# The first matmul of both MLPs as seven half-sized products, with the weights stationary, interleaved with the second matmul

## The chip, the cores and the metric

The kernel runs on one core of a Trainium2 chip, as one launch. The metric is the time of one execution on the device in microseconds (us), lower is better. Before the change three runs took 1429.39 to 1430.68 us, median 1429.62 us. A profile of one execution shows each engine: TensorE (PE, with its weight loads as PEld), VectorE (DVE), ScalarE (ACT), GpSimd (POOL) and the DMA queues that SyncE (SP) and GpSimd feed.

## The reference

A two-layer encoder over 512 positions of width 1024, in float32. Layer 0 mixes tokens with dilated sliding-window attention in three head groups, layer 1 with multi-head latent attention. Each mixer is followed by a squared-ReLU MLP:

```python
def rms_norm(x, gain):
    y = xf * lax.rsqrt(jnp.mean(xf * xf, axis=-1, keepdims=True) + EPS)
    return (y * gain.astype(jnp.float32)).astype(x.dtype)

def sq_relu_mlp(h, w1, w2):
    a = jax.nn.relu(h @ w1)
    return (a * a) @ w2

for i in range(DEPTH):                      # DEPTH = 2
    h = rms_norm(x, norm_mix[i])
    x = x + (dilated_mixer(h, ...) if i % 2 == 0 else mla_mixer(h, ...))
    h = rms_norm(x, norm_ffn[i])
    x = x + sq_relu_mlp(h, ffn_w1[i], ffn_w2[i])   # w1 1024 x 4096, w2 4096 x 1024
```

The change is in how `h @ w1` is computed, with what it needs around it.

## The kernel before

**Float32 by three matmuls.** Every float32 operand of a projection is split into two float32r parts: ACT copies the rounded part `hi`, DVE subtracts to get `lo` (lines 157 and 158 for raw weights, 795 and 796 for the weights of the second matmul, 757 and 758 for its other operand). A product is then hi.hi + hi.lo + lo.hi, three matmuls into one PSUM bank. The tiles `whi` and `wlo` have four buffers of 128x1024, `raw` has three.

**Order.** The kernel is written with a tile framework: all loops are unrolled, and a planner with a cost model decides, at build time, the order of instructions on each engine, as far as the dependences and the free buffers allow. Each engine then works strictly in that order, and the semaphores follow from it. The order in the source acts as priority. `tc.issue_after(ins)` makes what a block puts on the engine of `ins` come after `ins` there.

**The start of an MLP.** `project` (line 909) multiplies the mixer's output by its out-projection in two column halves. As each of the four token blocks of the second half ends, DVE adds it to the residual (line 915), and `norm_tile` (line 214) takes the mean square (ACT), the root (POOL), the scaled rows (DVE, line 220) and eight transposes (PE, line 124), and splits the result into `hT` (lines 228 and 229).

**The MLP** (`mlp`, line 868) takes the 4096 hidden columns in four chunks of 1024. `up(ch, grp)` computes 512 hidden columns, transposed: the weights are stationary, 128 columns at a time, and all 512 tokens stream past, so a group is 4 x 8 x 3 = 96 matmuls of 512 columns. The first group of each MLP goes by token halves (256 columns, 192 matmuls), since the halves become ready one after the other. ACT applies ReLU and squares (lines 891, 892) into `a2`. There are eight groups in a layer.

`down(ch)` calls `wino` (line 761), the second matmul for one chunk. It views the 512 x 1024 by 1024 x 1024 product as 2 x 2 blocks and uses seven products in place of eight (Winograd's form of Strassen's scheme). A product is 24 matmuls of 512 columns (line 852) with the activations stationary. Sums of activation blocks are made on DVE (line 789), sums of weight blocks by accumulating DMAs on POOL's queue (line 781), and the products are added to the residual by DVE (line 826). The weight blocks lie in four slots of `wqs`. The last chunk has its own order of products, so that token blocks end early.

The source order is up(ch+1, 0), down(ch), up(ch+1, 1); the planner sets few matmuls of the one between those of the other.

**The v projection** of layer 0 (`v_phase`, line 307 on) already uses the seven products for its weights in `piece`: sums of weight blocks are made there on DVE by `add_block` (line 334), the splits are at lines 386, 387, 406 and 407, the matmuls at line 421, the results go through `put` (lines 438, 440, 444).

**The last pair of heads** of layer 1 (`score`, lines 1114 to 1121): scores on PE, maximum on DVE, Exp on ACT. The matmuls of the out-projection's first half that need only earlier heads are set between by the planner.

Of the kernel before, what the change touches and what calls it, by code (L numbers as in the profile page):

```python
# [87 lines left out]
def encoder_kernel(ctx: ExitStack, tc: tile.TileContext, x, norm_mix, norm_ffn, a_w_qkv, a_q_gain, a_k_gain,  # L88
# [7 lines left out]
    def nm(s):  # L96
        uid[0] += 1
        return f"{s}_{uid[0]}"
# [208 lines left out]
    def v_phase(vp):  # L307
# [447 lines left out]
    def split_a(x, pool):  # L755
        t = pool.tile([P, 4, 2, 256], F32R, tag="asp", name=nm("asp"), bufs=4)
        A.activation(t[:, :, 0], x, AF.Copy)
        V.tensor_tensor(t[:, :, 1], x, t[:, :, 0].bitcast(F32), op=ALU.subtract)
        return t

    def wino(tag, Aq, w, wqs, pool, resid, done=None):
# [24 lines left out]
        def stmp(name, x, y, op):  # L786
            if name not in S:
                S[name] = pool.tile([P, 4, 256], F32, tag="S", name=nm("S"), bufs=2)
            V.tensor_tensor(S[name], x, y, op=op)
            return S[name]  # L790
# [14 lines left out]
        b7 = fetch(s7, (1, 1), add=True)  # L805

        def operands(p):
            if p == 5:
                return stmp("c", Aq(1, 0), Aq(1, 1), ALU.subtract), bT
            if p == 1:  # L810
                return Aq(0, 0), b1
            if p == 3:
                stmp("d", S["c"], Aq(0, 0), ALU.subtract)
                return stmp("c", S["d"], Aq(0, 1), ALU.add), b3
            if p == 6:
                return S["d"], fetch(sT, (1, 1), add=True)
            if p == 7:
                return stmp("c", Aq(0, 0), Aq(1, 0), ALU.subtract), b7
# [10 lines left out]

        banks = {}  # L830
        for p, chain, first, (i, n, op) in ORDER if done is None else ORDER_LAST:
            a, wq = operands(p)
            at = split_a(a, pool)
# [20 lines left out]
            put(i, n, op, bk)  # L854


    SLOTS = [(0, 1, 2, 3)]
    for _ in range(3):
# [3 lines left out]
    ORDER = [(1, "a", True, (0, 0, ALU.add)), (5, "b", True, (1, 1, ALU.add)), (3, "b", False, (0, 1, ALU.add)),  # L862
             (6, "a", False, (0, 1, ALU.subtract)), (2, "d", True, (0, 0, ALU.add)),
             (7, "a", False, (1, 1, ALU.subtract)), (4, "a", False, (1, 0, ALU.add))]

    ORDER_LAST = [ORDER[0], ORDER[4]] + ORDER[1:4] + ORDER[5:]

    def mlp(layer, w1, w2, hT_m, resid, pool, done):
        a2s = {}

        wqs = big.tile([P, 8, 2, 512], F32, tag="hT", name=nm("wqs"))

        def up(ch, grp):
            if grp == 0:
                if ch % 2:
                    a2s[ch] = pool.tile([P, 8, S], F32, tag="a2", name=nm("a2"))
                else:
                    a2s[ch] = x16.tile([P, 8, S], F32, tag="x16", name=nm("a2"))
            a2 = a2s[ch]
            c0 = ch * 1024 + grp * 512  # L880
            first = c0 == 0

            def mm(o, kt, hi, lo, hv, n=256 if first else 512):
                wh, wl = hi[:, o * P:(o + 1) * P], lo[:, o * P:(o + 1) * P]
                sl = slice(hv * n, hv * n + n)
                hh, hl = hT_m[:, kt, 0, sl], hT_m[:, kt, 1, sl]
                return [(wh, hh, sl), (wh, hl, sl), (wl, hh, sl)]

            def evac(o, acc):
                f = grp * 4 + o  # L890
                A.activation(a2[:, f], acc, AF.Relu)
                A.activation(a2[:, f], a2[:, f], AF.Square)

            run_block(w_units(w1, c0, 512), [4] if first else [1] * 4, 512, mm, evac, halves=2 if first else 1)

        def down(ch):
            a2 = a2s.pop(ch)
            wino(layer * 4 + ch, lambda i, j: a2[:, 4 * j:4 * j + 4, 256 * i:256 * i + 256],
                 w2[1024 * ch:1024 * ch + 1024, :], wqs, pool, resid, done if ch == 3 else None)
# [9 lines left out]
    def project(o_hl, w, resid, gain_src, hT_n, pool, g_name, begun=None):  # L909

        gain = gain_table(gain_src, D, g_name)
        for c in range(2):
            def evac(r, acc, c=c):
                sl = resid[:, r, 512 * c:512 * c + 512]
                V.tensor_tensor(sl, sl, acc, op=ALU.add)  # L915
                if c == 1:
                    norm_tile(r, resid[:, r], gain, hT_n, pool)
# [13 lines left out]
    hT = h1.tile([P, KD, 2, S], F32R, name="hT_f0")  # L931
# [3 lines left out]
    with tc.tile_pool(name="mlp0", bufs=1, reuse_waits="tile") as mp:  # L935
        state = {}

        def done0(r, c):
            state[r] = state.get(r, 0) + 1
            if state[r] < 2:  # L940
                return
            if r == 0:
                state["g"] = gain_table(norm_mix[1:2, :].rearrange("o d -> (o d)"), D, "g_mix1")
                state["hT"] = new_hT()
            norm_tile(r, resid[:, r], state["g"], state["hT"], mp, xn_tag="S")
        mlp(0, ffn_w1[0], ffn_w2[0], hT, resid, mp, done0)
# [4 lines left out]
    if True:  # L951
        with tc.tile_pool(name="bpool", bufs=1, reuse_waits="tile") as bp, \
# [153 lines left out]
            def score(d, h, r):  # L1106
# [9 lines left out]
                V.tensor_reduce(mx[:, 0:1], sc, axis=AX.X, op=ALU.max)  # L1116
                V.tensor_scalar(mx[:, 1:2], mx[:, 0:1], rq, -1.0, op0=ALU.mult, op1=ALU.mult)
                pe = bw.tile([P, S], F32, tag="pe", name=nm("pe"), bufs=3)
                A.activation(pe, sc, AF.Exp, bias=mx[:, 1:2], scale=rq, accum_out=mx[:, 2:3])
# [69 lines left out]
    hT = bh.tile([P, KD, 2, S], F32R, name="hT_f1")  # L1189
    with tc.tile_pool(name="po1", bufs=1, reuse_waits="tile") as po:  # L1190
# [36 lines left out]
```

## Time and profile before

| | before |
|---|---|
| median of 3 runs | 1429.62 us |
| the profiled execution | 1427.53 us, span 1425.8 us, TensorE's granted clock 1.00 |
| PE, PEld busy | 98%, 83% of the span |
| DVE, ACT, POOL busy | 66%, 52%, 15% |
| DMA | 185.25 MB, mean 130 GB/s |

The span runs from the first to the last instruction. An engine's busy time is the union of its instructions. Matmuls overlap in PE's pipeline, so the time that a row gives for one is longer than the distance to the next. Idle time stands beside the instruction that it precedes, with what ended it. L185 is the line of the shared matmul helper for projections and for the first matmul of the MLPs; the tiles tell them apart (`hT_f` is the MLP's).

### The profile page before, as it was taken

What the parts mean: (1) busy time and instruction counts of PE and PEld (TensorE: products, weight loads), DVE (VectorE), ACT (ScalarE), POOL (GpSimd) and SP (SyncE); (2) the same over time, 40 slices, a digit from 0 to 9 for tenths busy, and PEclk for the clock granted to TensorE, in tenths of its full rate; (3) what the DMA queues carried; (4) which work ended last, traced back from release to release, by engine and by line L of the source; (5) the groups of instructions that cost most, each with busy time, mean ns of one, the idle gap of its engine ahead of it and who ended that gap; (6) DMA issues with size and microseconds to landing.
All of it is one profiled execution on the core that took longest, in us unless ns stands there. A gap on an engine that the chain in (4) does not pass through costs nothing.

```text
span 1425.8 us, 19234 instructions
## 1 busy us (share of the span) xinstructions
PE 1394.0 (98%) x7044; PEld 1183.8 (83%) x7044; DVE 939.6 (66%) x1497; ACT 740.5 (52%) x1594; POOL 217.2 (15%) x240
## 2 busy tenths in 40 slices
PE   7999999999999999999999999999999999999998
PEld 7999888988888988888888887777768888888886
DVE  6886768676886754465564759788745365575647
ACT  6554656464564623553545446677633553544543
POOL 1110212021112001020010203433201020020201
PEclk9999999999999999999999999999999999999999
DMA  9535222322322335668493844200115658394835
GB/s 323 166 134 168 75 87 87 107 89 75 118 61 77 121 134 195 174 133 222 116 233 99 206 120 91 82 31 30 44 40 163 183 127 231 93 234 128 192 90 118
DMA packets 121086, 185.25 MB, mean 130 GB/s; under 512 B 8416, under 2 KB 58336, under 8 KB 120992
## 3 DMA queue, kind: packets, MB, share of 16 engines
q1 hardware_dynamic: 101808, 144.96, 31.6%
q0 software_dynamic: 19184, 39.07, 15.2%
q8 instruction: 55, 0.90, 0.3%
q14 instruction: 39, 0.32, 0.1%
HBM read 176.13 MB, written 7.86 MB: 129 GB/s over the span
## 4 chain that ended last, share of the span: by engine, by line
PE 89%; DVE 6%; ACT 2%; issue 1%; DMA 1%; POOL 0%; SPq 0%; DVEq 0%; ACTq 0%; POOLq 0%
PE acc L185 51%; PE sc L852 11%; PE tp L852 7%; PE tp L124 4%; PE sc L421 3%; PE acc L1138 1%; PE sc L1032 1%; PE acc L1114 1%; PE tp L421 1%; DVE wlo L796 1%; PE sco L701 1%; PE sc L587 1%; PE acc L421 1%; PE sco L697 1%; DVE wlo L407 1%
## 5 line engine op out<-in xcount | busy, mean ns | idle before, releaser
L185 PE MATMUL acc<-whi,hT 128*128 128x512 f32 (+2 forms) x1216 | 384.2, 390 | 2.2 <-ACT hT L739 1.3
L185 PE MATMUL acc<-hT_f,whi 128*128 128x512 f32 (+1 forms) x1152 | 318.7, 366 | 1.7 <-DVE resid L915 1.2
L158 DVE TENSOR_TENSOR wlo<-raw,whi 128x1024 fp32r<-128x1024 f32 (+3 forms) x146 | 172.4, 1189 | 180.2 <-ACT whi L157 179.9
L185 PEld LDWEIGHTS acc<-whi,hT 128*128 128x128 f32 x1216 | 225.4, 188 | 42.0 <-ACT hT L739 1.9
L185 PEld LDWEIGHTS acc<-hT_f,whi 128*128 128x128 f32 x1152 | 208.1, 189 | 37.4 <-DVE resid L915 1.6
L185 PE MATMUL acc<-wlo,hT 128*128 128x512 f32 (+2 forms) x608 | 235.9, 388 | 0.0
L157 ACT ACTIVATE whi<-raw 128x1024 fp32r<-128x1024 f32 (+3 forms) x146 | 149.7, 1031 | 161.5 <-PE acc L185 64.1
L796 DVE TENSOR_TENSOR wlo<-wqs,whi 128x1024 fp32r<-128x1024 f32 x112 | 137.9, 1232 | 113.4 <-ACT whi L795 113.4
L185 PE MATMUL acc<-hT_f,wlo 128*128 128x512 f32 (+1 forms) x576 | 204.9, 366 | 0.0
L795 ACT ACTIVATE whi<-wqs 128x1024 fp32r<-128x1024 f32 x112 | 118.8, 1061 | 161.3 <-PE acc L185 65.8
L852 PE MATMUL sc<-whi,asp 128*128 128x512 f32 x512 | 164.9, 390 | 0.8 <-DVE resid L826 0.7
L781 POOL DMA_DIRECT2D wqs<-in_ffn_w_dram x64 | 77.6, 1344 | 546.1 <-DVE wlo L796 362.4
L185 PEld LDWEIGHTS acc<-wlo,hT 128*128 128x128 f32 x608 | 114.4, 188 | 18.7 <-issue 0.2
L185 PEld LDWEIGHTS acc<-hT_f,wlo 128*128 128x128 f32 x576 | 108.5, 189 | 17.4
L852 PE MATMUL tp<-whi,asp 128*128 128x512 f32 x352 | 112.2, 390 | 1.8 <-DVE resid L826 1.8
L852 PEld LDWEIGHTS sc<-whi,asp 128*128 128x128 f32 x512 | 96.1, 188 | 21.4 <-issue 1.5
L132 POOL TENSOR_TENSOR qrs<-rs_v,nhalf 128x4 f32<-128x4 f32 x48 | 58.7, 1228 | 288.8 <-DVE rs_v L129 239.7
L852 PE MATMUL sc<-wlo,asp 128*128 128x512 f32 x256 | 99.6, 389 | 0.0
L137 ACT ACTIVATE junk<-acc 128x128 f32<-128x128 f32 x192 | 53.0, 276 | 56.4 <-PE acc L185 51.4
L852 PEld LDWEIGHTS tp<-whi,asp 128*128 128x128 f32 x352 | 66.1, 188 | 16.4 <-DVE resid L826 2.7
L852 PE MATMUL tp<-wlo,asp 128*128 128x512 f32 x176 | 68.2, 389 | 0.0
L295 ACT ACTIVATE qkT<-tp 128x512 f32<-128x512 f32 x48 | 35.8, 765 | 51.2 <-PE tp L124 50.9
(231 smaller groups left out, 2185.3 us busy)
## 6 DMA issues: line engine op xcount, KB each, us to landing
wqs<-in_ffn_w_dram SPq DMA_DIRECT2D x80, 512.0 KB, 5.1
raw<-in_ffn_w_dram SPq DMA_DIRECT2D x64, 512.0 KB, 4.5
wqs<-in_ffn_w_dram POOLq DMA_DIRECT2D x64, 512.0 KB, 7.5
raw<-in_a_w_qkv_dram SPq DMA_DIRECT2D x96, 256.0 KB, 3.1
b<-in_a_w_qkv_dram SPq DMA_DIRECT2D x24, 384.0 KB, 5.7
vall<-vo POOLq DMA_DIRECT2D x24, 192.0 KB, 2.2
raw<-in_a_w_o_dram SPq DMA_DIRECT2D x8, 512.0 KB, 3.8
raw<-in_b_w_o_dram SPq DMA_DIRECT2D x8, 512.0 KB, 3.7
```

What stands on the lines that cost most here:

```text
L124: PE.transpose(o, i, ident)
L132: G.tensor_tensor(out, v[:, :n], nhalf[:, :n], op=ALU.pow)
L137: A.activation(junk, x, AF.Square, scale=1.0 / math.sqrt(dim), accum_out=out)
L157: A.activation(hi[:, :nk, :n], raw[:, :nk, :n], AF.Copy)
L158: V.tensor_tensor(lo[:, :nk, :n], raw[:, :nk, :n], hi[:, :nk, :n].bitcast(F32), op=ALU.subtract)
L185: PE.matmul(accs[o][:, oc], lhsT=lt, rhs=rt, start=(kt == 0 and p_i == 0 and hv == 0), stop=(kt == total - 1 and p_i == 2), skip_group_che ...
L295: A.activation(dst, tv, AF.Copy)
L421: PE.matmul(banks[t][:, :VH], lhsT=lt, rhs=rt[:, j], start=(first and k == 0 and i_ == 0), stop=(k == 3 and i_ == 2), skip_group_check=True)
L781: marks["sum"] = nc.gpsimd.dma_start(t, src, accum_op=ALU.add).ins
L795: A.activation(hi, x, AF.Copy)
L796: V.tensor_tensor(lo, x, hi.bitcast(F32), op=ALU.subtract)
L852: PE.matmul(bk[t], lhsT=lt, rhs=rt[:, j], start=(first and k == 0 and i_ == 0), stop=(k == 3 and i_ == 2), skip_group_check=True)
```

## The change

The first matmul now uses the seven products too. The 512 tokens, the 1024 input features and a group's 512 hidden columns are each halved; a product is 256 hidden columns by 512 features by 256 tokens: 2 x 4 x 3 = 24 matmuls of 256 columns, weights stationary. A group makes seven products, 168 matmuls.

- `project` builds the seven token-side operands (four blocks, three further sums; `norm_blocks`) while it normalises, as tile `H` of seven split blocks, in place of `hT`. Products 1 and 2 need token blocks 0 and 1 alone.
- Class `Up` holds one group: four weight blocks of 512 KB (one in a tile `wk`, three in `raw`), four weight sums on DVE in place, a split for each product, and three PSUM banks (chains a, b, d). Three results are copied out by ACT, three are added out of PSUM by DVE, and ReLU and the square follow.
- `mlp` starts with group 0 and product 1 of group 1, and then writes out an order of single products: those of the two groups of the next chunk, with those of `wino`, now a generator that yields after each product, set between. The order of `wino`'s products is now 1, 5, 6, 3, 7, 2, 4 (before: 1, 5, 3, 6, 2, 7, 4); that of the last chunk stays.
- `wino`'s split operands have two buffers (before four). The sums of products 5 and 3 are made in halves, with less room. `a2` has three homes of half the size in place of two.
- In the v projection's first piece the sum that product 4 needs is made by an accumulating DMA on POOL's queue, not by DVE.
- In layer 1 what `project` puts on DVE and ACT comes after the maximum and the Exp of the last pair's first score.

```diff
@@ piece, in v_phase
-            add_block(bT[g], bT[g], b21[g])
+            if g:
+                add_block(bT[g], bT[g], b21[g])
+            else:
+                for u in range(2):
+                    nc.gpsimd.dma_start(bT[g][:, 2 * u:2 * u + 2], wblk(g, 1, 0, u), accum_op=ALU.add)
@@ wino
+        def sums(p, t):
...
+                    if p == 5:
+                        V.tensor_tensor(d, part(Aq(1, 0), u), part(Aq(1, 1), u), op=ALU.subtract)
+                        split_to(part(t, u), d)
+                        V.tensor_tensor(d, d, part(Aq(0, 0), u), op=ALU.subtract)
+                    else:
+                        c = pool.tile([P, 2, 256], F32, tag="S", name=nm("S"), bufs=1)
+                        V.tensor_tensor(c, d, part(Aq(0, 1), u), op=ALU.add)
+                        split_to(part(t, u), c)
...
-            at = split_a(a, pool)
+            at = asps[asp_n[0] % 2]
...
             put(i, n, op, bk)
+            yield
...
+    class Up:
+        CHAIN = {1: "a", 6: "a", 7: "a", 4: "a", 5: "b", 3: "b", 2: "d"}
...
+        def rest(self):
+            for key in ((1, 0), (0, 1), (1, 1)):
+                t = wp.tile([P, 2, 512], F32, tag="raw", name=nm("raw"), bufs=3)
+                self.w[key] = self.load(key, t.rearrange("p k (h n) -> p (k h) n", h=2))
+        def weight(self, p):
+            w = self.w
+            T = w[0, 0]
+            if p == 5:
+                V.tensor_tensor(T, T, w[0, 1], op=ALU.add)
+            if p == 6:
+                V.tensor_tensor(T, T, w[1, 1], op=ALU.add)
+            if p == 7:
+                V.tensor_tensor(w[0, 1], w[0, 1], w[1, 1], op=ALU.add)
+            if p == 4:
+                V.tensor_tensor(T, T, w[1, 0], op=ALU.add)
+            return w[{3: (1, 1), 7: (0, 1), 2: (1, 0)}.get(p, (0, 0))]
...
+        def product(self, p):
+            x = self.weight(p)
...
+            A.activation(hi, x, AF.Copy)
+            V.tensor_tensor(lo, x, hi.bitcast(F32), op=ALU.subtract)
...
+            for o in range(2):
+                for k in range(4):
+                    wh, wl = hi[:, k, o * P:(o + 1) * P], lo[:, k, o * P:(o + 1) * P]
+                    for i_, (lt, rt) in enumerate(((wh, H[:, k, 0]), (wh, H[:, k, 1]), (wl, H[:, k, 0]))):
+                        PE.matmul(acc[:, 256 * o:256 * o + 256], lhsT=lt, rhs=rt,
...
+            if p == 1:
+                A.activation(self.block(0, 0), av, AF.Copy)
...
+            else:
+                c, op = {2: (self.block(0, 0), ALU.add), 3: (self.block(0, 1), ALU.add),
+                         7: (self.block(1, 1), ALU.subtract)}[p]
+                V.tensor_tensor(c, c, av, op=op)
+                self.end(c, c)
@@ mlp
-        up(0, 0)
-        up(0, 1)
-        for ch in range(3):
-            up(ch + 1, 0)
-            down(ch)
-            up(ch + 1, 1)
-        down(3)
+        g0 = group(0)
+        g0.rest()
+        g0.product(1)
+        g0.product(2)
+        g1 = group(1)
+        g1.product(1)
+        for p in (5, 6, 3, 7, 4):
+            g0.product(p)
+        g1.rest()
+        for p in (5, 6, 3, 7, 2, 4):
+            g1.product(p)
+        for ch in range(3):
+            d = down(ch)
+            for h, plan in ((2 * ch + 2, (0, 1, 5, 0, 6, 3, 0, 7, 2, 0, 4, 0, 0)),
+                            (2 * ch + 3, (1, 5, 6, 0, 3, 7, 2, 0, 4))):
+                g = group(h)
+                g.rest()
+                for p in plan:
+                    if p:
+                        g.product(p)
+                    else:
+                        next(d)
+        for _ in down(3):
+            pass
@@ project, norm_blocks (replaces norm_tile here)
+                if r < 2:
+                    parts_of(1 + half, i, tv)
+                    A.activation(h32[:, i, 4 * half:4 * half + 4], tv, AF.Copy)
+                elif half:
+                    A.activation(dif[:, 0, i], tv, AF.Copy)
+                    parts_of(4, i, tv)
+                else:
+                    V.tensor_tensor(dif[:, 0, i], tv, dif[:, 0, i], op=ALU.subtract)
+                    V.tensor_tensor(dif[:, 1, i], h32[:, i, 0:4], tv, op=ALU.subtract)
+            if r >= 2:
+                c = dif[:, 0, i]
+                parts_of(5, i, c)
+                V.tensor_tensor(c, c, h32[:, i, 0:4], op=ALU.subtract)
+                parts_of(6, i, c)
+                V.tensor_tensor(c, c, h32[:, i, 4:8], op=ALU.add)
+                parts_of(3, i, c)
+                parts_of(7, i, dif[:, 1, i])
@@ layer 1
+                    if s_ == HB * NT - 8:
+                        last_pair = marks["max"], marks["exp"]
...
-    with tc.tile_pool(name="po1", bufs=1, reuse_waits="tile") as po:
+    with tc.tile_pool(name="po1", bufs=1, reuse_waits="tile") as po, \
+            tc.issue_after(last_pair[0]), tc.issue_after(last_pair[1]):
```

More of the change, by code (lines that the diff above doesn't have):

```diff
@@ L752, in encoder_kernel, with split_to, wino @@
     ap0.__exit__(None, None, None)
-    def split_a(x, pool):
-        t = pool.tile([P, 4, 2, 256], F32R, tag="asp", name=nm("asp"), bufs=4)
+    def split_to(t, x):
         A.activation(t[:, :, 0], x, AF.Copy)
         V.tensor_tensor(t[:, :, 1], x, t[:, :, 0].bitcast(F32), op=ALU.subtract)
-        return t
-    def wino(tag, Aq, w, wqs, pool, resid, done=None):
+    def wino(tag, Aq, w, wqs, asps, pool, resid, done=None):
         v = w.rearrange("(k p) c -> p k c", p=P)
@@ L832, in wino @@
             a, wq = operands(p)
[L833 removed]
+            at = asps[asp_n[0] % 2]
+            asp_n[0] += 1
+            if a is None:
+                sums(p, at)
+            else:
+                split_to(at, a)
             if first:
@@ L909, in project @@
-    def project(o_hl, w, resid, gain_src, hT_n, pool, g_name, begun=None):
-        gain = gain_table(gain_src, D, g_name)
+    ORDER = [(1, "a", True, (0, 0, ALU.add)), (5, "b", True, (1, 1, ALU.add)), (6, "a", False, (0, 1, ALU.subtract)),
+             (3, "b", False, (0, 1, ALU.add)), (7, "a", False, (1, 1, ALU.subtract)), (2, "d", True, (0, 0, ALU.add)),
+             (4, "a", False, (1, 0, ALU.add))]
+    ORDER_LAST = [ORDER[n] for n in (0, 5, 1, 3, 2, 4, 6)]
+    H_OF = {1: 0, 2: 1, 4: 2, 5: 3, 6: 4, 3: 5, 7: 6}
@@ new lines, in mlp, with group, down @@
+    def mlp(layer, w1, w2, H, resid, pool, done):
+        wqs = big.tile([P, 8, 2, 512], F32, tag="hT", name=nm("wqs"))
+        asps = pool.tile([P, 2, 4, 2, 256], F32R, name="asp")
+        a2c = pool.tile([P, 4, S], F32, name="a2")
+        a2ab = x16.tile([P, 2, 4, S], F32, tag="x16", name=nm("a2"))
+        homes = [a2ab[:, 0], a2ab[:, 1], a2c]
+        def group(h):
+            return Up(w1, 512 * h, H, homes[h % 3], pool)
+        def down(ch):
+            a2s = [homes[(2 * ch + j) % 3] for j in range(2)]
+            return wino(layer * 4 + ch, lambda i, j: a2s[j][:, :, 256 * i:256 * i + 256],
+                        w2[1024 * ch:1024 * ch + 1024, :], wqs, [asps[:, n] for n in range(2)], pool, resid,
+                        done if ch == 3 else None)
+        g0 = group(0)
[18 more added lines that the diff above has]
+                        g.product(p)
+                    else:
+                        next(d)
+        for _ in down(3):
+            pass
@@ L916, in evac @@
                 if c == 1:
-                    norm_tile(r, resid[:, r], gain, hT_n, pool)
+                    norm_blocks(r)
             if c == 0 and begun is not None:
```

119 lines of the change are left out of this document (76 added, 43 removed).

## The prediction

> **What bounds the kernel now.** I read the page first, then the stretches of the MLPs, then the groups with their shapes apart, last the chain of waits.
>
> ```profile
> span 1425.8 us, 19234 instructions
> PE 1394.0 (98%) x7044; PEld 1183.8 (83%) x7044; DVE 939.6 (66%) x1497; ACT 740.5 (52%) x1594; POOL 217.2 (15%) x240
> ...
> PE 89%; DVE 6%; ACT 2%; issue 1%; DMA 1%; POOL 0%; SPq 0%; DVEq 0%; ACTq 0%; POOLq 0%
> ```
>
> TensorE is busy for 98% of the span and is 89% of the chain that ended last. What shortens the kernel is less work on PE, as long as PE is still fed. The next rows are one steady chunk of the second MLP (both groups of the first matmul and one second matmul).
>
> ```profile
> 1241.00:1322.00 81.00, 81.00 (x359) 67.09 (x358) 47.84 (x47) 38.93 (x45) 9.72 (x8) 1.00 0.66 168
> ```
>
> Columns: PE, PEld, DVE, ACT, POOL, granted clock, DMA share, GB/s. PE never rests (81.00 of 81.00, clock 1.00); VectorE works 47.84 us, 59%, ScalarE 48%.
>
> **Term 1, the matmuls removed.** The groups of the first matmul in the MLPs, and pieces of the chain that give the pace of matmuls in a row:
>
> ```profile
> L185 PE MATMUL acc<-hT_f,whi 128*128 128x512 f32 x896 | 270.8, 389 | 0.0
> L185 PE MATMUL acc<-hT_f,wlo 128*128 128x512 f32 x448 | 169.1, 389 | 0.0
> L185 PE MATMUL acc<-hT_f,whi 128*128 128x256 f32 x256 | 48.0, 287 | 1.7 <-DVE resid L915 1.2 <-ACT hT_f L228 0.5
> L185 PE MATMUL acc<-hT_f,wlo 128*128 128x256 f32 x128 | 35.8, 283 | 0.0
> ```
>
> ```profile
> 252.32 1.79 PE sco L697 x16
> ...
> 555.76 2.88 PE acc L185 x24
> ...
> 620.32 5.44 PE sc L852 x24
> ```
>
> The mean of one (389, 287 ns) is a latency, since matmuls overlap; the pace is 5.44/24 = 226.7 ns for 512 columns and 2.88/24 = 120.0 ns for 256. Half the columns cost 53% of the time, and this is already a weight-stationary 256-column stream with a new weight for every matmul, the very form that the change uses. The 16 matmuls of 128 columns keep 1.79/16 = 112 ns: there the columns no longer set the pace, so I take 112 ns as the floor that a new weight puts under a matmul. 120 lies just above it. Before: (896+448) x 226.7 + (256+128) x 120.0 = 304.6 + 46.1 = 350.7 us. After: 16 groups x 7 products x 24 = 2688 matmuls of 256 columns x 120.0 = 322.6 us. **Minus 28.1 us**; the second matmul keeps its count.
>
> [...]
>
> **Term 2, feeding PE in the steady part.** What DVE and ACT do there, one by one (last numbers: busy, mean ns | idle before):
>
> ```profile
> L158 DVE TENSOR_TENSOR wlo<-raw,whi 128x1024 fp32r<-128x1024 f32 x128 | 155.5, 1224 | 177.3 <-ACT whi L157 177.0
> L796 DVE TENSOR_TENSOR wlo<-wqs,whi 128x1024 fp32r<-128x1024 f32 x112 | 137.9, 1232 | 113.4 <-ACT whi L795 113.4
> L157 ACT ACTIVATE whi<-raw 128x1024 fp32r<-128x1024 f32 x128 | 134.9, 1059 | 157.1 <-PE acc L185 63.8 <-PE sc L852 49.1 <-DMA raw<-in_ffn_w_dram 20.6
> L892 ACT ACTIVATE a<-a 128x512 f32<-128x512 f32 x64 | 40.4, 632 | 2.0
> ```
>
> ```profile
> 525.50 1.28 DVE L915 TENSOR_TENSOR resid<-resid,acc 128x512 f32<-128x512 f32 x2 [1.70 <-PE acc L185]
> ...
> 547.52 3.49 DVE L158 TENSOR_TENSOR wlo<-raw,whi 128x1024 fp32r<-128x1024 f32 x3
> ```
>
> In a row these overlap a little: with the single durations (1.22 and 0.68) taken off, a further one adds (3.49 - 1.22)/2 = 1.14 us at 1024 elements and 0.60 us at 512. A new group gives DVE 7 splits and 4 weight sums (11 x 1.14) and 3 additions out of PSUM (3 x 0.60) = 14.3 us, against 4 splits = 4.6 us now. One second matmul: 14 weight splits, 5 whole operand splits and the whole sum of product 7 (20 x 1.14), 10 half-sized sums and splits of products 5 and 3 and 14 additions to the residual (24 x 0.60) = 37.2 us. Chunk: 2 x 14.3 + 37.2 = 65.8 us of DVE in 2 x 20.16 + 38.08 = 78.4 us of PE: **84%**, from 59%. ACT: two groups of 7 x 1.06 + 11 x 0.63, and 19 x 1.06 + 4 x 0.63 = 51.4 us, 66%; it follows PE and DVE and I cost it at nothing (without slack it would be late with hi, rival (b)). No such mix stands in this trace at 84%; the nearest rows are the v projection, also made of seven products with sums on DVE:
>
> ```profile
> 30.00:64.00 34.00, 32.52 (x188) 31.63 (x187) 31.66 (x43) 19.97 (x32) 4.40 (x7) 1.00 0.61 197
> 64.00:126.00 62.00, 61.38 (x352) 60.70 (x351) 46.93 (x59) 32.55 (x47) 9.21 (x18) 1.00 0.36 126
> ```
>
> DVE at 76% leaves PE idle 1.0%, at 93% 4.4%. Of 6 chunks x 78.4 = 470 us, nothing is the one end and 2.6% (the line between the rows at 84%), 12 us, the other. I take 1.5%, **plus 7 us**, nearer to the 76% row because here two independent streams of products lie beside each other, and one covers what the other waits for.
>
> The interleaving adds waits for PSUM: product 6 goes onto the bank of product 1, and 7 onto that of 6. Each has another product between, 2.88 us, which hides one read of the bank (0.63 us and its hand-over). Nothing, therefore; without cover it would be about 1 us each.
>
> **Term 3, the start of each MLP.** The norm now makes seven operands out of each token block.
>
> ```profile
> 550.93 0.68 DVE L915 TENSOR_TENSOR resid<-resid,acc 128x512 f32<-128x512 f32 x1
> 551.53 1.28 DVE L229 TENSOR_TENSOR hT_f<-tp,hT_f 128x512 fp32r<-128x512 f32 x2
> ...
> 555.98 1.28 DVE L220 SCALAR_TENSOR_TENSOR xn<-resid,nrs,g_ffn 128x1024 f32<-128x1024 f32 x1
> ```
>
> ```profile
> 552.68 0.36 PE L185 MATMUL acc<-hT_f,whi 128*128 128x256 f32 x1
> ```
>
> ```profile
> 880.91 0.87 PE tp L124 x8
> ```
>
> PE begins steadily at 552.68, once token blocks 0 and 1 are split, and so it will. Three products (1, 2, and 1 of the next group) need only those; with them, products 5, 6, 3 and 16 transposes (2 x 0.87 us) PE comes to product 7 at 552.7 + 6 x 2.88 + 1.7 = 571.7. DVE has from 551.5: 2 x 0.60 (block 1), 2 x 9 x 0.60 (blocks 2, 3: five splits and four sums), 1.2 for the last xn, 7 x 1.14 for the weights of 5, 6, 3, 7 and 2 x 0.60 for additions = 22.4 us, to 573.9. That is 2.2 us late without a gap, and after the late step the same products are due. I take 3 us for each layer, **plus 6 us**; ends 1 us less than now (the wait before 552.68 was there already) and 7 us (all of block 2 and 3 served before product 5, and gaps).
>
> **Term 4, the edges.** The out-projection of layer 1 now queues behind the first maximum and Exp of the last pair of heads.
>
> ```profile
> 1016.22 1.11 ACT L157 ACTIVATE whi<-raw 128x1024 fp32r<-128x1024 f32 x1
> ...
> 1025.81 0.77 ACT L1119 ACTIVATE pe<-sc,bmx,rqs 128x512 f32<-128x512 f32 x1
> ```
>
> ```profile
> 1018.60:1025.80 7.20, 5.28 (x18) 3.41 (x19) 1.00 0.21 73
> ```
>
> The last row counts L185 alone: 18 matmuls of the projection, 18 x 0.227 = 4.1 us, fill PE ahead of that Exp. They move behind it. Queued behind the held split are the projection's later splits on ACT and DVE, and for those only PE's filling waits. At worst 4.1 us are lost; at best the attention, no longer interrupted, comes 1.1 us earlier (that one split). I take **plus 1.5**.
>
> In the v projection, two sums of bT leave DVE for an accumulating DMA:
>
> ```profile
> 50.47 1.82 DVE L334 TENSOR_TENSOR bT<-bT,b 128x768 f32<-128x768 f32 x2
> ```
>
> ```profile
> 56.38 0.41 PE L421 MATMUL sc<-whi,Ssp 128*128 128x384 f32 x1 [1.40 <-DVE vo L440]
> wqs<-in_ffn_w_dram POOLq DMA_DIRECT2D x64, 512.0 KB, 7.5
> ```
>
> DVE is full there, so up to the 1.40 us wait can go; the transfer (7.5 us for 512 KB, ours is 384) with two issues on POOL may land up to some 1.5 us after product 4 wants it, my estimate. On POOL they stand ahead of the stores of `vo`, which nothing near waits for. I take **minus 0.5**. The second matmul of the last chunk has two operand buffers for four, with DVE at 37.2 of 38.08 us; it waits once now:
>
> ```profile
> 1399.86 0.50 PE L852 MATMUL tp<-whi,asp 128*128 128x512 f32 x1 [0.92 <-DVE resid L826]
> ```
>
> I take 1 us for each layer, **plus 2** (ends minus 0.9 and plus 3 each).
>
> **Sum.** -28.1 + 7 + 6 + 1.5 - 0.5 + 2 = -12.1 us. The profiled execution took 1427.53 us (span 1425.8 and 1.7 around it): 1415.4. The median of the runs, 1429.62, is 2.1 higher: **1417 us**.
>
> **Rivals.** (a) PE is fed throughout. Terms 2 and 4 vanish and the start costs 1 us a layer: -28.1 + 2 = -26, 1404 us. For it: DVE stays below its time everywhere but at the start. Against: 4.4% at 93%.
>
> (b) Slower: DVE waits for ACT's hi at each weight split, in the steady chunks. Today it does so for 113.4/112 = 1.01 us. With 28 splits in a chunk, 65.8 + 28 x w must stay under 78.4 us, so it binds from w = 0.45 us; the whole gain (28.1 less 9 elsewhere, over 6 chunks 3.2 us) is gone at w = 0.56. At 0.6: 65.8 + 16.8 = 82.6, 4.2 x 6 = 25 us in place of 7, +6 us in all: 1436 us; at 1.01 some 75 us worse than now. Against it, the same step where DVE is full:
>
> ```profile
> L407 DVE TENSOR_TENSOR wlo<-b,whi 128x768 fp32r<-128x768 f32 x24 | 22.7, 954 | 11.7 <-ACT whi L406 11.6
> L407 DVE TENSOR_TENSOR wlo<-bT,whi 128x768 fp32r<-128x768 f32 x18 | 17.2, 953 | 2.9 <-ACT whi L406 2.8
> ```
>
> (11.7 + 2.9)/42 = 0.35 us: a wait shrinks when there is other work.
>
> (c) Weights come late. The three raw buffers are reloaded only after the sum of product 4, and product 5 of the next group wants the second of the three loads:
>
> ```profile
> raw<-in_ffn_w_dram SPq DMA_DIRECT2D x64, 512.0 KB, 4.5
> ```
>
> Each group still takes four loads of 512 KB on SP, in rows half as long. I estimate 4.5 us and half again for the second, 6.8, then sum, hi and lo, 3.4: 10.2 us. The cover is two products (4, and 1 of the next group, 5.8 us) and what that sum runs ahead, up to three products (8.6 us): enough at two, 0.9 us late at one and a quarter. 14 hand-overs x 0.9 = 12.6 us: 1430 us, no change.
>
> (d) The weight load shows at 256 columns after all, so the change doesn't do what it says: 960 x 112 ns = +107 us on top: 1525 us. The rows of term 1 speak against it. [...]
>
> **How the numbers follow.** Forecast 0.65 (own range 1408 to 1426: terms 2 and 3, 13 us together, off by 70% either way), (a) 0.15, (c) 0.07, (b) 0.12, (d) 0.01. The range runs from 1402, within (a), to 1433, below most of (b). All terms at their ends together give 1395 to 1439. Within 0.2% (2.9 us) is about what a measurement can't tell from no change: (c) and the upper edge of the forecast, 0.08. Faster: the rest of the forecast and (a), 0.78. Slower: (b), (d) and some of (c), 0.14.
>
> **What would show it.** Right: 2688 matmuls of 256 columns at 120 ns in a row; a chunk of 78 to 80 us with DVE at 82 to 86%; PE waits of 2 to 4 us between 552 and 576. Wrong: chunks above 81 us with DVE idle behind ACT's hi (b) or behind raw (c); a pace over 125 ns (d); PE idle in 1018 to 1030 for more than 4 us (term 4). A chunk under 78.5 us with a start that costs nothing is (a).

## The result: slower, 1466.36 us

The changed kernel took 1466.36 us (median of 4 runs, 1464.91 to 1468.57), the kernel before in the same comparison 1429.51. The ratio is 1.0259, interval 1.0246 to 1.0272: **slower by 2.6%**, 49 us above the forecast and 33 above the end of the range. The page of the profile after:

```profile
span 1464.7 us, 21654 instructions
...
PE 1379.9 (94%) x8004; PEld 1215.0 (83%) x8004; DVE 1112.1 (76%) x1723; ACT 824.2 (56%) x1730; POOL 217.8 (15%) x242
...
PE 81%; DMA 8%; DVE 5%; ACT 3%; issue 2%; SPq 0%; POOL 0%; ACTq 0%; DVEq 0%
```

PE is busy for 14.1 us less than before (1394.0), but idle for 84.8 us in place of 31.8, 53.0 more: the span is 38.9 us longer. DMA, 1% of the chain before, is 8% now. The idle time is not spread out. PE's waits, grouped (total, times, longest; the row left out, 8.7 us near the kernel's start, was 8.4 before):

```profile
PE acc L963 <- ACT whi L951: 34.9, 3, 18.0
...
PE tp L124 <- DVE xn L220: 5.6, 1, 5.6
PE tp L124 <- ACT h L1054: 4.5, 2, 2.3
PE tp L124 <- DVE dif L1060: 3.6, 2, 1.8
PE sc L1271 <- ACT pe L1276: 2.8, 1, 2.8
```

The first four rows shown, 48.6 us in all, are not there before the change, where 3.3 us of other waits stood at the start of the two MLPs; the second of them stands at the end of layer 0, the others at the start of the two MLPs. The last is a wait in the attention of layer 1, also new.

**The steady part is as forecast.** A chunk, by the windows and by the same piece of the chain in two chunks:

```profile
766.43:844.90 78.47, 78.47 (x506) 71.73 (x505) 67.35 (x73) 48.36 (x59) 9.65 (x8) 1.00 0.67 166
```

```profile
1243.52 8.39 PE acc L963 x70
...
1322.07 8.39 PE acc L963 x70
```

PE never rests, 8.39/70 = 119.9 ns a matmul, 78.55 us a chunk (1322.07 - 1243.52), DVE at 86%.

**The start of the first MLP**, windows, then SP's queue, ACT and PE:

```profile
552.00:574.00 22.00, 3.09 (x16) 2.41 (x16) 12.52 (x20) 9.03 (x16) 5.45 (x5) 0.57 1.07 298
574.00:580.00 6.00, 5.67 (x28) 5.38 (x29) 4.99 (x5) 3.08 (x4) 0.00 (x0) 0.57 0.39 90
```

```profile
549.46 4.01 SPq L788 DMA_DIRECT2D wqs<-in_ffn_w_dram  x8
553.81 2.94 SPq L919 DMA_DIRECT2D wk<-in_ffn_w_dram  x2
```

```profile
573.07 1.06 ACT L951 ACTIVATE whi<-wk 128x1024 fp32r<-128x1024 f32 x1 [7.72 <-DMA wk<-in_ffn_w_dram]
```

```profile
574.18 0.80 PE L963 MATMUL acc<-hT_f,whi 128*128 128x256 f32 x2 [16.73 <-ACT whi L951]
```

The first product begins at 574.18, not at 552.68 as forecast. The first weight block (`wk`) of groups 0 and 1 is issued behind eight loads for the second matmul of the first chunk, 4 MB that must wait until PE has ended the out-projection (SP idles 20.3 us for it); it then shares the DMA engines with them and with accumulating loads from POOL's queue (DMA share 1.07, 298 GB/s). The other three blocks of group 0 (`raw`) had been loaded long before. In the 22 us PE does the norm's 16 transposes, and the granted clock is 0.57, in the 6 us behind it too. Layer 1 shows the same, with 18.0 us and a clock of 0.64 behind it (1138 to 1144).

**The end of layer 0**, DVE, then PE:

```profile
890.59 1.22 DVE L801 TENSOR_TENSOR d<-a 128x1024 f32<-128x1024 f32 x1
```

```profile
888.21 1.97 PE L124 MATMUL tp<-ck,xn 128*128 128x128 f32 x8 [5.61 <-DVE xn L220]
...
893.48 0.80 PE L885 MATMUL sc<-whi,asp 128*128 128x512 f32 x1
```

Product 6 of the last second matmul ended at 882.6, product 7 starts at 893.48. Its operand sum `d` is a tile of the tag `wk` with two buffers, and the norm of the next layer takes its `xn` from the same two. `d` stands behind two of those, and waits until block 0 has been normalised and transposed.

### The profile page after: what moved, and what is told of

Read it like the earlier page. It is cut to its first block, busy times and chain, and to the rows that moved or that the text cites. A ratio compares the mean times of both kernels' runs of the same rounds, so it can differ in the third digit from the quotient of the medians.

```text
span 1464.7 us, 21654 instructions
## 1 busy us (share of the span) xinstructions
PE 1379.9 (94%) x8004; PEld 1215.0 (83%) x8004; DVE 1112.1 (76%) x1723; ACT 824.2 (56%) x1730; POOL 217.8 (15%) x242
## 4 chain that ended last, share of the span: by engine, by line
PE 81%; DMA 8%; DVE 5%; ACT 3%; issue 2%; SPq 0%; POOL 0%; ACTq 0%; DVEq 0%
PE acc L185 26%; PE acc L963 19%; PE sc L885 11%; PE tp L885 7%; PE tp L124 3%; DMA wk<-in_ffn_w_dram 3%; PE sc L421 2%; DMA wqs<-in_ffn_w_dram 2%; PE acc L1295 1%; PE acc L1271 1%; PE sc L1189 1%; PE tp L421 1%; PE sco L706 1%; PE sc L592 1%; PE sco L702 1%
## 5 line engine op out<-in xcount | busy, mean ns | idle before, releaser
L963 PE MATMUL acc<-hT_f,whi 128*128 128x256 f32 x1792 | 328.5, 285 | 35.1 <-ACT whi L951 34.9
L963 PEld LDWEIGHTS acc<-hT_f,whi 128*128 128x128 f32 x1792 | 284.6, 194 | 40.2 <-ACT whi L951 36.5
L963 PE MATMUL acc<-hT_f,wlo 128*128 128x256 f32 x896 | 253.1, 284 | 0.4 <-DVE wlo L952 0.4
L963 PEld LDWEIGHTS acc<-hT_f,wlo 128*128 128x128 f32 x896 | 172.4, 193 | 1.2 <-DVE wlo L952 0.8
L823 DVE TENSOR_TENSOR wlo<-wqs,whi 128x1024 fp32r<-128x1024 f32 x112 | 137.2, 1228 | 26.9 <-ACT whi L822 26.9
L158 DVE TENSOR_TENSOR wlo<-raw,whi 128x1024 fp32r<-128x1024 f32 (+3 forms) x82 | 94.3, 1160 | 55.6 <-ACT whi L157 55.3
L157 ACT ACTIVATE whi<-raw 128x1024 fp32r<-128x1024 f32 (+3 forms) x82 | 82.3, 1009 | 57.5 <-PE acc L185 21.7
L952 DVE TENSOR_TENSOR wlo<-wk,whi 128x1024 fp32r<-128x1024 f32 x64 | 78.3, 1224 | 41.3 <-ACT whi L951 41.3
L951 ACT ACTIVATE whi<-wk 128x1024 fp32r<-128x1024 f32 x64 | 67.7, 1059 | 62.3 <-DMA wk<-in_ffn_w_dram 20.5
```

The source lines that it names most:

```text
L157: A.activation(hi[:, :nk, :n], raw[:, :nk, :n], AF.Copy)
L158: V.tensor_tensor(lo[:, :nk, :n], raw[:, :nk, :n], hi[:, :nk, :n].bitcast(F32), op=ALU.subtract)
L823: V.tensor_tensor(lo, x, hi.bitcast(F32), op=ALU.subtract)
L951: A.activation(hi, x, AF.Copy)
L952: V.tensor_tensor(lo, x, hi.bitcast(F32), op=ALU.subtract)
L963: PE.matmul(acc[:, 256 * o:256 * o + 256], lhsT=lt, rhs=rt, start=(first and o == 0 and k == 0 and i_ == 0), stop=(o == 1 and k == 3 and i ...
```

## The experiments

Each run was timed with the kernel before on the same chip (1428.2 to 1428.8 us there). The last column is the ratio less 1.0259, in us of 1428.6. A typical interval, 0.0015 either way, is 2.1 us, so that two runs less than some 3 us apart can't be told apart.

| run | edit | us | ratio (95%) | against the change |
|---|---|---|---|---|
| e1 | wqs behind wk on SP | 1455.37 | 1.0193 (1.0174-1.0211) | -9.4 |
| e2 | wk in the operands' pool | 1455.47 | 1.0191 (1.0175-1.0206) | -9.7 |
| e3 | d in a raw buffer | 1455.59 | 1.0196 (1.0181-1.0211) | -9.0 |
| e4 | e2 + e3 | 1446.58 | 1.0125 (1.0110-1.0140) | -19.1 |
| e5 | e4, norm ahead of weights | 1438.28 | 1.0066 (1.0049-1.0083) | -27.6 |
| e6 | e4, wqs behind raw | 1438.13 | 1.0063 (1.0046-1.0080) | -28.0 |
| e7 | e5 + e6 | 1452.58 | 1.0168 (1.0152-1.0184) | -13.0 |
| e8 | not interleaved | 1467.04 | 1.0271 (1.0256-1.0286) | +1.7 |
| e9 | e4, finer order | 1436.28 | 1.0055 (1.0040-1.0070) | -29.1 |
| e10 | e9, weight sums on POOL | 1438.48 | 1.0075 (1.0051-1.0100) | -26.3 |
| e11 | e10, no hold | 1438.42 | 1.0071 (1.0047-1.0096) | -26.9 |
| e12 | no hold | 1459.83 | 1.0226 (1.0209-1.0243) | -4.7 |
| e13 | e9, no hold | 1429.81 | 1.0007 (0.9998-1.0017) | -36.0 |
| e14 | e13, a fourth product first | 1423.62 | **0.9964** (0.9951-0.9976) | -42.1 |
| e15 | e13, DVE work left out (another result) | 1425.75 | 0.9979 (0.9970-0.9988) | -40.0 |

### Is the first weight block late by its place, by its memory, or not at all?

```diff
 e1, in mlp: the first step of the first second matmul
+with tc.issue_after(g1.first_ins):      # g1's load of wk
     next(d)
 e2: wk from the pool that is opened before the out-projection
-pool.tile([P, 4, 256], F32, tag="wk", ...)
+wkp.tile([P, 4, 256], F32, tag="wk", ...)     # wkp = h1, bh in layer 1
```

> Only the order on SP's queue is changed: the eight loads of the first second matmul (wqs) are issued behind the first blocks of weights (wk) of the first two groups, in both layers. Theory 1 (place in the queue): the first product, which starts at 574.2 us in layer 0 now, waits only because wk stands behind 4 MB. wk is then issued at about 549.5 and lands 5 to 7 us later, the first product starts at 556 to 558, 17 us earlier a layer and with less of the slow clock behind it: 1466.4 - 36 = about 1430 us. Theory 2 (memory): wk's buffer lies where the out-projection's pool has xn, so that the load, once it is ahead, waits for the last transpose of the norm (about 557 to 560): first product at 563 to 567, 7 to 11 us earlier a layer, 1444 to 1452 us. Theory 3 (my prediction's: DVE's work on the norm sets the start, not a load): no change, 1466.

> The two wk buffers move from the pool of the MLP (opened after the out-projection) to the pool that holds the operands hT_f and is opened before it; nothing else changes. Theories 1 and 2 (wk comes late, by its place in the queue or by its memory): the loads go out with those of raw, before the out-projection ends, and the first product starts as soon as token blocks 0 and 1 are split, at 552 to 556 in layer 0, 18 to 22 us earlier a layer, and the 3 to 4 us of slow clock after the idling go too: 1466.4 - 2 x 22 = 1422 us (1416 to 1430). What is then left of PE's idling before the steady part is what my term 3 spoke of, 2 to 4 us a layer. Theory 3 (the norm's work on DVE): no change, above 1460.

In both runs `wk` came early, and both gained a quarter of what theory 1 had (9.4 of 36, 9.7 of 44). In e1 SP issues it 25 us earlier, but ACT's order still has its split behind the whole norm (SP, ACT, PE):

```profile
528.86 1.06 SPq L919 DMA_DIRECT2D wk<-in_ffn_w_dram  x2
```

```profile
565.13 1.04 ACT L953 ACTIVATE whi<-wk 128x1024 fp32r<-128x1024 f32 x1
```

```profile
566.22 0.80 PE L965 MATMUL acc<-hT_f,whi 128*128 128x256 f32 x2 [8.90 <-ACT whi L953]
```

The load was issued 36 us before, and none of its kind took over 9.8 us in this run: it was there for 26 us at least. 566.2 lies in the window of theory 2, whose mechanism was wrong: the memory was free. In e2 the planner sets the block's split ahead of the norm's last work, and the first product starts at 550.09; now PE waits for the norm (PE; PE's waits from 545 to 620; DVE):

```profile
550.09 0.99 PE L963 MATMUL acc<-hT_f,whi 128*128 128x256 f32 x3 [0.25 <-ACT hT_f L1037]
```

```profile
PE acc L963 <- ACT hT_f L1037: 6.9, 3, 4.6
PE acc L963 <- DVE hT_f L1038: 5.2, 3, 2.1
```

```profile
577.40 1.23 DVE L931 TENSOR_TENSOR wk<-wk,raw 128x1024 f32<-128x1024 f32 x1 [3.38 <-DMA raw<-in_ffn_w_dram]
578.54 0.68 DVE L1064 TENSOR_TENSOR dif<-dif,h 128x512 f32<-128x512 f32 x1
```

DVE works on weights of products 5, 6 and 7 first, and at 577.40 a sum that waits for the second group's `raw` stands in front of the norm's last sums. So the late load is shown to be a cause, and it hid a second one. "No change" (theory 3) falls, but what it named, the norm on DVE, is what waits next.

### Does the shared buffer hold product 7?

```diff
-d = pool.tile([P, 4, 256], F32, tag="wk", name=nm("d"), bufs=2)
+d = wp.tile([P, 2, 512], F32, tag="raw", ...)   # seen as 4 x 256
```

> In the last second matmul of layer 0 and 1, the sum d of product 7 gets a buffer of raw (idle there) in place of one of the two wk buffers, which the norm of the next layer takes for its xn. Theory A (shared buffer): product 7 started at 893.5, 11 us after product 6 ended at 882.5, because d waited until xn of token block 0 had been transposed. With its own buffer product 7 follows product 6 at once: 9 to 12 us less in layer 0, nothing in layer 1: 1455 us. Theory B (the gain table is loaded late, at 873.2, and the norm takes its time anyhow; product 7 only moves ahead of it and the wait stands behind): 0 to 3 us less, 1464 us.

> Both: wk in the pool of the operands, and d of product 7 in a buffer of raw. If the two losses are separate and both causes are right, the gains add up: 1466.4 - 44 - 11 = 1411 us (1403 to 1420), faster than the kernel before (1429.5). If one of them only uncovers the other (the wait moves elsewhere), less than the sum: above 1420.

Theory A: product 7 starts at 886.58 (893.48 in the change), and the run is 9.0 us shorter. The norm's transposes now start at 896.49, behind product 7 and half of product 4:

```profile
886.58 0.47 PE L885 MATMUL sc<-whi,asp 128*128 128x512 f32 x1 [2.78 <-DVE resid L853]
```

e4 gains 19.1 where the parts gave 9.7 + 9.0: two separate losses. Its forecast (1411) fell with e2's.

### The order of work at the start

```diff
 e5, e9: each product's work on its weights behind the norm's split of an operand for token block 3
+with tc.issue_after(norm_split_act), tc.issue_after(norm_split_dve):
     g0.product(p)          # e5: behind the split for p; e9: for the product before p (for 5: xn)
 e6, e7: the wqs loads behind the second group's raw
+with tc.issue_after(last_raw):
     next(d)
```

> On top of e4: in the first group of each MLP the work on the weights of products 5, 6, 3 and 7 (sum, hi, lo) is queued on ACT and DVE behind the norm's split of the same product's operand for token block 3, and that of product 4 and of the second group behind the last of these splits. Theory P (order on DVE): e4 still loses 13 us of idling PE between 550 and 586, and a clock of 0.5 to 0.72 in 553 to 586 with it, because four sums and splits of weights stand ahead of the splits of block 1 (ready at 553.1), block 2 and block 3, and because at 577.4 a sum that waits for a DMA stands ahead of the last of them. With the norm first, products 1, 2 and 1 of the next group run from 550, product 5 starts at 561 to 564 and is followed without a long wait: 10 to 14 us less a layer, 1446.6 - 24 = 1422 us (1415 to 1430). Theory Q (amount): DVE has simply too much to do there whatever the order, and what is put first makes the other late: 0 to 4 us a layer, above 1438.

> On top of e4, the order on SP alone: the eight wqs loads are issued behind the three raw loads of the second group, in both layers. Theory P: the sum at 577.4 that waits 3.4 us for raw starts as soon as raw, issued at 564.6, has landed in the 4.6 us that such a load takes when the engines are free, at about 570; the splits behind it come 3 to 4 us earlier, and the clock rises earlier: 3 to 6 us less a layer, 1446.6 - 9 = 1437 us (1433 to 1442). If the transfer wasn't what ended the wait: no change, 1446; if wqs then comes late for the second matmul, slower.

> e5 and e6 together. Theory P: both orders right, the start costs what my term 3 had put on it, 1 to 5 us a layer: 1412 to 1420 us, 1416 in the middle, and faster than the kernel before (1428.6). Theory Q: as e6, 1437, or later.

e5 gave 8.5 us beyond e4, a third of theory P's 24 and on the edge of theory Q. e6 gave 8.9, as expected. Together (e7) they are 6.1 us slower than e4: the held weight work lets the second group's `raw` go late, so that the 4 MB behind it are issued from 579.06 on (570.07 in e6), and the third group's `raw`, issued at 591.61 behind them, becomes a step of the chain of waits (17.77 us in layer 1):

```profile
593.88 16.67 DMA raw<-in_ffn_w_dram
```

In each place on SP's queue that was tried for the 4 MB, something waited behind them; they did least harm where nothing was due. In e5 DVE had idled while product 5's sum stood behind the norm (DVE, then PE):

```profile
557.64 0.69 DVE L1063 TENSOR_TENSOR dif<-tp,dif 128x512 f32<-128x512 f32 x1 [3.18 <-ACT dif L1060]
```

```profile
568.68 0.79 PE L963 MATMUL acc<-hT_f,whi 128*128 128x256 f32 x2 [5.02 <-ACT whi L951]
571.67 0.58 PE L963 MATMUL acc<-hT_f,wlo 128*128 128x256 f32 x1 [2.19 <-DVE wlo L952]
```

> As e5 (on top of e4), but each product's work on its weights is queued one step earlier: that of product 5 behind block 3's xn, of 6 behind the norm's splits for 5, of 3 behind those for 6, of 7 behind those for 3, of 4 and of the second group behind those for 7. In e5 product 5 started at 568.7, 5.0 + 2.2 us after the first three products, because its sum stood behind the norm's split (566.3) while DVE had idled 3.2 us before 557.6. Theory P (order): product 5 starts at 564 to 566, the later ones wait 1 us at most, the clock stays up: 6 to 8 us less a layer than e5's 1438, so 1424 (1418 to 1431). Theory Q (DVE's work, 22 us for 10 us of cover, sets the time whatever the order): 1434 or above.

Product 5 then starts at 564.81 as expected, yet the gain over e5 is 1.5 us only, too little to tell from none. The later products wait for their own operands, 1 to 2 us each:

```profile
564.81 0.38 PE L963 MATMUL acc<-hT_f,whi 128*128 128x256 f32 x1 [1.99 <-ACT hT_f L1045]
...
570.81 0.39 PE L963 MATMUL acc<-hT_f,whi 128*128 128x256 f32 x1 [1.29 <-DVE hT_f L1046]
...
576.53 0.38 PE L963 MATMUL acc<-hT_f,whi 128*128 128x256 f32 x1 [1.21 <-ACT hT_f L1045]
```

Theory P's starting time was right, its gain was not; Q's bound (1434 or above) holds.

### Amount, cover, or the next load?

```diff
 e10: G.tensor_tensor in place of V.tensor_tensor for the first group's four sums
 e14: product 2 of the second group ahead of product 5 of the first
+far = wqs[:, 2 * SLOTS[(layer * 4) % 4][3] + 1]    # seen as 4 x 256
+g1.w[1, 0] = g1.load((1, 0), far)
+g1.product(2, True)
 e15: the norm's eight sums for blocks 2, 3 and the first group's four sums left out
```

> e9 with the four sums of weights of the first group (products 5, 7, 6, 4) on POOL in place of DVE, in both layers, and POOL's accumulating loads of the second matmul behind them. A sum of 256 elements takes 0.74 us on POOL here, so one of 1024 about 2.5 to 3 us (my estimate); POOL is idle but for the three small nrs. It takes 4.6 us a layer from DVE. If DVE's amount is what is left of the loss: 2 to 4 us a layer less than e9, about 1418. If the order was all: as e9. If POOL's longer sums come late, or slow DVE down: slower than e9.

> e13 with a fourth product that needs only token blocks 0 and 1 ahead of product 5: product 2 of the second group; its block of weights is loaded into one of wqs's buffers that the second matmul takes up last. The second group's other products now also wait for the norm's splits for product 3. Theory 'PE lacks cover while DVE makes the operands of blocks 2 and 3': each layer gets 2.9 us more of it and, with shorter pauses, 1 to 2 us less of slow clock: 8 to 9 us less than e13, 1424 us (1419 to 1430), below the kernel before (1428.7). Theory 'something later than the norm ends the wait, such as raw of the second group': no gain, 1431 or above.

> e13 with work left out at the start of each MLP: the eight sums of the norm for token blocks 2 and 3 and the four sums of weights of the first group are not computed (the splits read what is there), so the result is another; 8 x 0.60 + 4 x 1.14 = 9.4 us a layer come off DVE. If DVE's amount is what holds PE back there: 6 to 10 us a layer less than e13, 1417 us (1411 to 1424). If it is the chain of hand-overs (xn, transposes, copies on ACT, hi, lo): 0 to 3 us a layer, 1428 or above.

e10 is not faster than e9. POOL's sums come late, and they stretch DVE's work (POOL, then DVE):

```profile
553.41 2.41 POOL L934 TENSOR_TENSOR wk<-wk,raw 128x1024 f32<-128x1024 f32 x1
555.90 3.28 POOL L938 TENSOR_TENSOR raw<-raw,raw 128x1024 f32<-128x1024 f32 x1
560.34 2.77 POOL L936 TENSOR_TENSOR wk<-wk,raw 128x1024 f32<-128x1024 f32 x1 [1.16 <-DVE wlo L955]
569.67 5.73 POOL L940 TENSOR_TENSOR wk<-wk,raw 128x1024 f32<-128x1024 f32 x1 [6.57 <-DVE wlo L955]
```

```profile
553.49 3.41 DVE L1061 SCALAR_TENSOR_TENSOR xn<-resid,nrs,g_ffn 128x1024 f32<-128x1024 f32 x1 [0.67 <-POOL nrs L132]
556.82 0.68 DVE L1074 TENSOR_TENSOR dif<-tp,dif 128x512 f32<-128x512 f32 x1
...
561.38 2.27 DVE L1053 TENSOR_TENSOR hT_f<-dif,hT_f 128x512 fp32r<-128x512 f32 x1
```

The scaled rows take 3.41 us in place of 1.28, a split 2.27 in place of 0.68, each while a sum runs on POOL: what DVE was spared is taken back.

e15 leaves out 9.4 us a layer of DVE's work, at the price of another result, and gains 2.0 a layer against e13. In its profile (of the longest of ten executions, 1429.43 us) the waits of products 5 to 4 are all but gone (one of 0.34 between 554 and 582), and then PE meets the next thing that is late, `raw` of the second group (SP, DVE, PE):

```profile
568.25 1.50 SPq L919 DMA_DIRECT2D raw<-in_ffn_w_dram  x2
```

```profile
580.53 1.23 DVE L937 TENSOR_TENSOR raw<-raw,raw 128x1024 f32<-128x1024 f32 x1 [6.11 <-DMA raw<-in_ffn_w_dram]
```

```profile
582.94 0.58 PE L965 MATMUL acc<-hT_f,wlo 128*128 128x256 f32 x1 [6.42 <-DVE wlo L954]
```

So DVE's amount is a cause. Behind it stand two things that the run doesn't separate: two of the three `raw` buffers are refilled only when the first group's splits have read them (568.25), and the sum that waits for the last load, product 7's, stands on DVE ahead of product 5's `lo`. The gain has the size of the second theory, but no chain of hand-overs shows; neither expectation met this. e14 leaves DVE its work and gives PE 2.9 us more to do meanwhile, which also takes one load out of that refill: 6.1 us less than e13 (8 to 9 were expected), and **faster than the kernel before** by 0.36%: little, but the interval lies below 1. Its cover and its earlier load were not tried apart.

### The hold, and the interleaving

```diff
 e11, e12, e13
 with tc.tile_pool(name="po1", ...) as po, \
-        tc.issue_after(last_pair[0]), tc.issue_after(last_pair[1]):
 e8: all seven products of the second matmul between the two groups
```

> The changed kernel without that hold, nothing else: 1.3 us less, 1465 us; the start of the second MLP is late by the wk load as before, so that what comes earlier may be lost there again: between 1462 and 1467.

> e10 without the hold on the out-projection of layer 1 (it is no longer queued behind the first maximum and Exp of the last pair of heads). My term 4 took the hold to cost 1.5 us (ends -1.1 and +4.1): 1.5 us less than e10; in the profile of the changed kernel the same milestones give 1.3.

> e9 without the hold on the out-projection of layer 1. Without the hold the projection's end came 5.4 us earlier in e12 (against the changed kernel) and 3.3 us earlier in e11 (against e10), where the start of the second MLP then gave most of it back. Here 2 to 4 us less than e9's 1436: 1433 us (1431 to 1437); if the start of the MLP takes all of it back, 1436.

> The changed kernel with the second matmul's seven products behind each other between the two groups, as the kernel before has them, in place of between the groups' products. Theory 'two streams cover each other': alone, the second matmul has 37.2 us of DVE in 38.08 us of PE, and its last, which runs alone today, loses 3.6 us in layer 1; six more that lose as much make 1466.4 + 6 x 3.6 = 1488 us (1480 to 1495). Theory 'the mean counts': the splits run ahead during the groups (14.3 of 20.2 us) and make up for it: within 4 us of 1466.

The same piece of the out-projection of layer 1, in the chains of the change and of e12:

```profile
1089.85 17.53 PE acc L185 x76
```

```profile
1084.41 17.53 PE acc L185 x76
```

Layer 0 ends 0.3 us earlier in e12, so the hold costs 5.1 us here. In time: 4.7 (e12) and 6.9 (e13 against e9), both more than expected, and 0.6 (e11 against e10, each uncertain by 3.5), where the start of the second MLP took part of it back: that piece starts 3.3 us earlier than in e10, the steady chunks 1.2.

e8 is within 1.7 us of the change, and in the same window its PE never rests either:

```profile
766.43:844.90 78.47, 78.47 (x507) 71.87 (x506) 66.86 (x73) 48.07 (x60) 9.63 (x8) 1.00 0.66 165
```

That PE is fed because two streams cover each other is refuted; the result fits the second theory, by which the splits run ahead during the groups. What the order as written adds can't be told from nothing.

## Why the prediction was wrong

**Term 1 was right, and it was not the time.** 119.9 ns against 120.0, 78.55 us a chunk against 78.4. Rivals (b) and (d) are out. (d) had put 112 ns on each of 960 additional weight loads (2688 - 1728); the page after has 960 more of them, one for each matmul (PEld x8004, PE x8004, both x7044 before), and the pace stays at 119.9 ns. PE's busy time fell by 14.1 us in place of 28.1; a part of the rest is the slow clock at the starts (28 matmuls take 5.67 us in 574 to 580, 3.4 at full pace), the remainder was not traced.

**Term 2 (7 us) was 0.** DVE's 84% was 86%, and in the steady chunks PE never waited for it. The v projection was the wrong row to lean on, and the reason for the lower value, two streams beside each other, was wrong too (e8).

**Term 3 is the step that failed**, in its first sentence: "PE begins steadily at 552.68, once token blocks 0 and 1 are split, and so it will." It counted DVE's work, and never asked when the operand on the other side arrives. `wk` is a new tile in a pool that opens after the out-projection, and it went behind eight loads on SP's queue; it was the queue that held it, since e1 issues it 25 us earlier into the same pool. I put 3 us on a layer; the waits there were 21.0 in layer 0 (16.9 + 2.3 + 1.8) and 22.1 in layer 1 (18.0 + 2.3 + 1.8), with a slow clock behind them (0.57 and 0.64).

Its count of DVE (22.4 us of work, 2.2 us late) was too kind as well: it assumed no gap and the best order. With the weights early the planner's order cost 12.1 us of waits (e2), and the best order found 8.3 (e9) before the fourth product. Rival (c), priced for the steady chunks, does not show there; at the start late `raw` is real (in the wait of 6.4 us in e15, a step of 16.67 us in e7).

**Term 4.** The hold was given 1.5 us, at worst 4.1: measured 4.7 to 6.9 where nothing took it back. The bound counted the 18 matmuls that filled PE, and not that PE then waits in the attention (2.8 us for one Exp, a wait that e12 doesn't have). The v projection's -0.5 was 0: PE is busy for 536.5 of the first 549.5 us before and after. The last second matmul was given 1 us a layer for its two operand buffers. Beside the 5.6 us its waits were 1.5 us in layer 0 and 4.5 in layer 1 (before 1.6 and 0.9), 3.5 us more in all where 2 were forecast; what makes the 4.5 was not traced. e3 shows 9.0 us in layer 0 from another shared buffer, which the prediction didn't look for, though one line of the kernel has it (`xn_tag="wk"`, before `"S"`; it is not among the lines of the diff shown).

**What the cures leave.** With all of them together (e14: load, order, cover, buffer, hold) the change is 5 us faster than before; the forecast had 12. A part of the missing 7 still stands at the two starts: PE waits there 5.2 and 5.4 us in e14, where term 3 had 3 each.

## What to carry to other kernels

When a change gives a stage new operands, ask for each of them which pool its buffer comes from, when that opens, and what stands ahead of its first load on the queue; "as before" holds only for what is loaded as before. Where several tiles share a tag, list who takes the buffers in the order of the source. At the start of a stage count, beside the amount of each in-order engine, the order in which it serves what, and try early what gave 6.1 us here (e14): more work for PE that needs nothing late.

## What the runs showed of the hardware

A pause of PE cost twice here: the wait, and a slower clock behind it. After 16.7 us of waiting in layer 0 the granted clock was 0.57 (row 574 to 580), and 28 matmuls took 5.67 us there. It was low behind shorter pauses too: 0.66 behind one of 2.1 us in e2, and in e5 0.52 behind one of 0.94 us (552 to 555) and 0.50 with those of 5.0 and 2.2 us (568 to 574). The rows of e2, then of e5:

```profile
553.00:558.00 5.00, 4.86 (x28) 4.86 (x29) 4.21 (x6) 1.58 (x3) 1.31 (x2) 0.66 1.03 384
```

```profile
552.00:555.00 3.00, 3.00 (x15) 3.00 (x16) 1.79 (x3) 1.08 (x2) 0.55 (x1) 0.52 1.06 408
568.00:574.00 6.00, 3.12 (x13) 2.83 (x14) 5.96 (x8) 1.88 (x3) 0.32 (x1) 0.50 0.81 139
```

The kernel before paused for 0.25, 0.72 and 0.22 us at the same place and kept a clock of 1.00:

```profile
552.00:555.00 3.00, 2.78 (x24) 2.73 (x24) 1.96 (x4) 2.24 (x4) 0.00 (x0) 1.00 0.96 336
```

No run varied the length of a pause alone.

DVE and POOL ran longer beside each other in e10, and not every operation did. Sums of 1024 elements took 2.41 to 5.73 us on POOL. Beside them two DVE operations with both operands in SBUF took 3.41 us (1.28 without) and 2.27 us (0.68 without), and one that reads PSUM (`tp`, at 556.82) kept its 0.68 us under a sum that ran from 555.90 to 559.18. Beside the last sum DVE's splits kept their times until 573 (1.21 us at 571.32), and it was the sum that took 5.73. No run moved an operand between SBUF and PSUM, so what decides which of the two is slowed is not shown.

A 512 KB load of the MLPs' weights lands 4.2 to 6.7 us after its issue in the median (`wqs` 4.2 from SP and 6.4 from POOL, `raw` 4.7, `wk` 6.7, in the change); the first `wk` took some 19 us (553.81 to 573.07) behind eight others, and in e1, issued ahead of them, no `wk` took over 9.8. The size was the same in both; the place on the queue was not.
